# Banks of their own for context blocks and value products, rotations behind the context's product, and a new order of loads in the second layer

## The chip, the cores and the metric

One core of a Trainium2 chip runs the whole program: a model of two layers over 512 latent tokens and 256 context tokens, 1024 channels, batch 1. The metric is the device time of one execution in microseconds (us). The kernel before takes 2702.51 us (median of 3 runs, 2702.22 to 2703.63).

## The reference

All data are float32. The parts that the change touches are the start of each layer and the attention.

```python
for l in range(DEPTH):                                  # DEPTH = 2
    last = l == DEPTH - 1
    sh1, sc1, gt1, sh2, sc2, gt2 = modulation(c, w_mod[l], b_mod[l])
    csh1, csc1, cgt1, csh2, csc2, cgt2 = modulation(c_ctx[None, :], w_mod[l], b_mod[l])
    h_lat = rmsnorm(x, g_norm1[l]) * (1.0 + sc1) + sh1
    h_ctx = rmsnorm(ctx, g_norm1[l]) * (1.0 + csc1) + csh1
    p_lat = h_lat @ w_in[l]
    if last:
        p_ctx_kv = h_ctx @ w_in[l][:, OFF_K:OFF_SC]     # the context's keys and values alone
    else:
        p_ctx = h_ctx @ w_in[l]
        p_ctx_kv = p_ctx[..., OFF_K:OFF_SC]
    k_ctx, v_ctx = keys_values(p_ctx_kv, k_gain[l])     # rmsnorm per head of 128
    q_lat = apply_rope(query_heads(p_lat, q_gain[l]), cos, sin)
    k_lat, v_lat = keys_values(p_lat[..., OFF_K:OFF_SC], k_gain[l])
    k_lat = apply_rope(k_lat, cos, sin)
    attn_lat = latent_attention(q_lat, k_lat, v_lat, k_ctx, v_ctx)
    x_new = x + gt1 * mixer_merge(p_lat, attn_lat, lp)
    h2 = rmsnorm(x_new, g_norm2[l]) * (1.0 + sc2) + sh2
    x_new = x_new + gt2 * squared_relu_mlp(h2, w_mlp_in[l], w_mlp_out[l])
    if not last:
        ...                                             # the same for the context, which reads only itself
    x = x_new
return rmsnorm(x, g_final)
```

There are 8 query heads and 2 key and value heads of 128 channels. The context's keys and queries carry no rotation.

## The kernel before, in words

**Products.** Every float32 operand of a large product is split into a high part (a cast to the matmul's reduced float32) and a low part (the rest), and `mm3` (lines 161 to 165) issues three matmuls for one product: high by high, the two mixed ones, all summed in PSUM. Weights come from HBM in units of 128 x 1024 numbers (512 KB) through four buffers (`wraw`, line 123). ScalarE (ACT) casts a unit (line 134), VectorE (DVE) or GpSimd (POOL) subtracts (line 136); four buffers each for the two parts. `w_qk` (line 475) loads a unit of the first query group's and the keys' columns in two DMAs, `qk_halves` splits it; there are four such units for a layer.

**PSUM.** A `PB` tile is one bank (512 columns, four of them in these stages), a `PA` tile two banks (1024 columns, two of them). In the two stages that matter here TensorE (PE) works with both.

**Other buffers.** SBUF tiles are taken by tag: tag A has 36 buffers, tag X 12 (token rows of 1024 columns, rotary tables, projections, probabilities, each call of `self.X`), tag `gt` (gate rows) 2, tag `gain` 2.

**Who orders.** The program is written as one sequence, partly through generators that are advanced a step at a time between other work (`coming`, `self.lat`, `ctx`, `self.bg`). A planner then sorts each engine's instructions: it simulates the engines, issues what is ready, prefers what is earlier in the program, and allots the tiles' buffers as it goes. `issue_after(x)` ties instructions: they may not be put in their queue before x has been put in its own. On the chip the order of each queue is then fixed. All loads in question stand in SyncE's queue (SP).

**The start of a layer.** Token rows are normalised (`norm_in`, line 1090: ACT sums the squares at 1093, POOL takes the root in `rstd` at 378 and 379, DVE scales at 1095). `modulate` (line 415) transposes the normalised rows on PE (428), and for each block of 128 channels ACT writes the modulated high part (433), ACT or DVE the whole (436 for odd blocks, 438 for even ones), DVE the low part (439). For the two blocks of context tokens a block of channels is 256 columns wide; with `wide` four such blocks share one PA, so two share a bank: one is transposed and read, then the next.

`qk_gemm_all` (line 484) multiplies all four latent blocks with the query and key columns, four banks open at once, and before products it advances `coming`, which is `first_in` in the first layer and `next_in` in the second; these make the modulated rows and the weights just ahead of their use. Then the context's product runs in one PA (lines 582 to 590).

**Rotations.** `rotary_in` (line 454) loads two gains and two copies of the rotary table (512 KB each, tag X). `rotary` (line 468) multiplies the tables by the gains on DVE. `qk_pair` (line 505) sums squares on ACT (512), and on DVE multiplies by the two halves of the table (522) and adds (525); `key` (551) then scales keys on POOL (555), `query` (559) leaves queries unscaled. The latents' two pairs of blocks are rotated ahead of the context's product in the program (lines 579 to 581), the context's pair behind it. `to_heads` (529) transposes the results into heads (534) and splits them.

**Attention.** `v_heads` (line 597) makes the values: three steps, each two products of 256 columns that share a PB bank, each split by ACT and DVE (156, 159). Two of the steps run before the first scores and one more between scores (732, 733, 738). `scores` (628) with part 2 are the context's own queries (first layer only): two products of 256 columns in one PB (651), each read before the next is written.

**Second layer's start.** It overlaps the end of the first layer's MLP. `finish` (1055) normalises each block as its last residual is done; the context's two blocks are the last two. `next_in` (1213) loads the four units of query and key weights, then the rotary tables, splits the weights, multiplies the tables, and modulates latents and context between products.

**Gate rows.** `gate_rows` (364) loads rows that multiply the output of a sub-layer into the residual (`residual`, 1112); the final norm's gain is loaded likewise at 1019. Both are plain loads on SP's queue.

## Time and profile before

| what | value |
|---|---|
| time, median of 3 runs | 2702.51 us (2702.22 to 2703.63) |
| the profiled execution's own time | 2700.5 us |
| its span | 2698.7 us |
| granted TensorE clock, mean over the span | 0.999 |
| PE busy | 2672.6 us |
| PEld busy (weight loads, beside PE) | 2300.5 us |
| DVE busy | 1624.6 us |
| ACT busy | 873.9 us |
| POOL busy | 693.3 us |
| DMA, mean over the span | 112 GB/s |

The profile is of one execution. PE is the engine of the matmuls, PEld its weight loads, DVE the vector engine, ACT the scalar engine, POOL GpSimd, SP the queue that issues most transfers. A line of a view names the line of the source (L163), the operation, and output<-inputs by the names of the tiles, and in brackets how long the engine stood idle ahead of it and what released it.

### The profile page before, as it was taken

How to read it: one execution, taken by the hardware profiler on the slowest of the kernel's cores; microseconds unless marked ns; L12 is line 12 of the kernel's file. 1: busy time of each engine (PE TensorE's matmuls, PEld its weight loads, DVE VectorE, ACT ScalarE, POOL GpSimd, SP SyncE). 2: the span in 40 equal slices, each digit the busy share in tenths (PEclk: the TensorE clock that was granted, in tenths of full speed). 3: DMA queues.
4: the chain of work that ended last, by engine and by line, in shares of the span. 5: the costliest groups of instructions: out<-in, count | busy, mean ns of one | idle time of the engine just before them, and what ended most of it. 6: DMA issues, size and time to landing. Idle time of an engine off the chain costs nothing.

```text
span 2698.7 us, 36188 instructions
## 1 busy us (share of the span) xinstructions
PE 2672.6 (99%) x14571; PEld 2300.5 (85%) x14571; DVE 1624.6 (60%) x2098; ACT 873.9 (32%) x1426; POOL 693.3 (26%) x593
## 2 busy tenths in 40 slices
PE   8999999999999999999999999999999999999998
PEld 5899888888888888888888888998888888888887
DVE  5656837897764335585445356657578645644545
ACT  4556222122212323412121235563223233422223
POOL 1433432243221220201010103335445212111102
PEclk9999999999999999999999999999999999999999
DMA  7211324432275243344334232114333634432332
GB/s 255 64 35 58 98 77 141 133 107 66 82 228 157 63 144 94 97 159 153 110 104 146 79 110 87 55 60 122 120 114 102 181 112 144 132 95 94 110 101 94
DMA packets 341983, 302.50 MB, mean 112 GB/s; under 512 B 10577, under 2 KB 288385, under 8 KB 341817
## 3 DMA queue, kind: packets, MB, share of 16 engines
q1 hardware_dynamic: 340400, 298.81, 35.8%
q8 instruction: 114, 1.87, 0.3%
q10 hardware_dynamic: 1416, 1.39, 0.2%
q14 instruction: 53, 0.43, 0.0%
HBM read 274.96 MB, written 25.20 MB: 111 GB/s over the span
## 4 chain that ended last, share of the span: by engine, by line
PE 96%; DVE 2%; DMA 1%; ACT 1%; issue 0%; POOL 0%; SPq 0%; POOLq 0%; ACTq 0%; DVEq 0%
PE pa L163 21%; PE pa L165 21%; PE pa L164 21%; PE pb L163 9%; PE pb L165 8%; PE pb L164 8%; PE pb L676 2%; PE pb L690 1%; PE pb L693 1%; PE pb L691 1%; DVE tx L522 1%; PE pa L428 0%; DVE wlo L136 0%; PE pb L918 0%; PE pb L784 0%
## 5 line engine op out<-in xcount | busy, mean ns | idle before, releaser
L163 PE MATMUL pa<-ta,whi 128*128 128x512 f32 (+1 forms) x2896 | 1023.9, 354 | 0.0
L164 PE MATMUL pa<-ta,wlo 128*128 128x512 f32 (+1 forms) x2896 | 1020.1, 352 | 0.0
L165 PE MATMUL pa<-ta,whi 128*128 128x512 f32 (+1 forms) x2896 | 1019.6, 352 | 0.0
L134 ACT CAST whi<-wraw 128x1024 fp32r<-128x1024 f32 x360 | 377.8, 1051 | 1036.5 <-PE pa L165 404.3
L163 PEld LDWEIGHTS pa<-ta,whi 128*128 128x128 f32 x2896 | 547.9, 189 | 78.5 <-issue 2.5
L165 PEld LDWEIGHTS pa<-ta,whi 128*128 128x128 f32 x2896 | 547.4, 189 | 75.0 <-DVE ta L439 0.2
L164 PEld LDWEIGHTS pa<-ta,wlo 128*128 128x128 f32 x2896 | 548.0, 189 | 73.4
L163 PE MATMUL pb<-whi,ta 128*128 128x512 f32 (+1 forms) x1200 | 435.2, 363 | 3.5 <-ACT ta L433 1.9
L165 PE MATMUL pb<-wlo,ta 128*128 128x512 f32 (+1 forms) x1200 | 432.5, 361 | 1.5 <-DVE wlo L136 1.5
L164 PE MATMUL pb<-whi,ta 128*128 128x512 f32 (+1 forms) x1200 | 432.9, 361 | 0.0
L760 DVE SCALAR_TENSOR_TENSOR pv<-tx,cols,pv 128x783 f32<-128x783 f32 (+1 forms) x448 | 400.9, 895 | 12.6
L136 DVE TENSOR_TENSOR wlo<-wraw,whi 128x1024 fp32r<-128x1024 f32 x248 | 322.7, 1304 | 89.3 <-ACT whi L134 83.5
L136 POOL TENSOR_TENSOR wlo<-wraw,whi 128x1024 fp32r<-128x1024 f32 x112 | 270.2, 2414 | 360.2 <-ACT whi L134 308.0
L163 PEld LDWEIGHTS pb<-whi,ta 128*128 128x128 f32 x1200 | 226.8, 189 | 41.7 <-ACT ta L433 2.6
L982 POOL TENSOR_TENSOR ta<-ta 128x768 fp32r<-128x768 f32 (+1 forms) x64 | 105.0, 1641 | 600.2 <-DVE ta L981 593.7
L165 PEld LDWEIGHTS pb<-wlo,ta 128*128 128x128 f32 x1200 | 226.7, 189 | 35.2 <-DVE wlo L136 1.7
L164 PEld LDWEIGHTS pb<-whi,ta 128*128 128x128 f32 x1200 | 227.0, 189 | 34.7 <-issue 0.8
L315 DVE SCALAR_TENSOR_TENSOR tx<-wraw,cs,tx 128x1024 f32<-128x1024 f32 x112 | 157.9, 1424 | 49.0 <-DMA wraw<-in_w_mod 44.1
L979 DVE TENSOR_SCALAR ta<-pa 128x512 f32<-128x512 f32 (+1 forms) x63 | 51.8, 822 | 192.5 <-PE pa L165 181.9
L1116 DVE TENSOR_TENSOR ta<-pb,gt 128x512 f32<-128x512 f32 x100 | 68.8, 688 | 160.0 <-PE pb L165 159.9
L803 ACT ACTIVATE ta<-pa 128x768 f32<-128x768 f32 (+1 forms) x52 | 36.6, 705 | 223.8 <-PE pa L165 215.1
L159 POOL TENSOR_TENSOR ta<-tx,ta 128x768 fp32r<-128x768 f32 (+1 forms) x32 | 52.6, 1643 | 156.2 <-ACT ta L156 151.7
(188 smaller groups left out, 2352.0 us busy)
## 6 DMA issues: line engine op xcount, KB each, us to landing
wraw<-in_w_in SPq DMA_DIRECT2D x144, 512.0 KB
wraw<-in_w_mod SPq DMA_DIRECT2D x80, 512.0 KB
wraw<-in_w_mlp_out SPq DMA_DIRECT2D x72, 512.0 KB
wraw<-in_w_mlp_in SPq DMA_DIRECT2D x64, 512.0 KB
wraw<-in_w_o SPq DMA_DIRECT2D x24, 512.0 KB
tx<-spill SPq DMA_DIRECT2D x24, 384.0 KB
ta<-in_w_mod SPq DMA_DIRECT2D x32, 256.0 KB
wraw<-in_w_attn_out SPq DMA_DIRECT2D x16, 512.0 KB
```

What stands on the lines that cost most here:

```text
L134: nc.scalar.copy(hi, raw)
L136: self.last_lo = self.lo_engine.tensor_tensor(lo, raw, hi.bitcast(F32), op=ALU.subtract)
L159: (eng or nc.gpsimd).tensor_tensor(lo, src, hi.bitcast(F32), op=ALU.subtract)
L163: nc.tensor.matmul(ps, ah, bh, start=start, stop=False)
L164: nc.tensor.matmul(ps, al, bh, start=False, stop=False)
L165: self.last_pe = nc.tensor.matmul(ps, ah, bl, start=False, stop=stop)
L315: nc.vector.scalar_tensor_tensor(acc[b], raw, c, acc[b], op0=ALU.mult, op1=ALU.add)
L676: nc.tensor.transpose(pt[:, b * 256 + q * P:b * 256 + (q + 1) * P], probs[n, part][q][:, o], self.ident)
L760: nc.vector.scalar_tensor_tensor((v if t == K_CF - 1 else pv)[:, 0:n], u[:, t:t + n], c["cf"](t, k), (v if t == 1 else pv)[:, 0:n], op0=AL ...
L979: nc.vector.tensor_scalar(out=v[:, 0:n], in0=ps[:, 0:n], scalar1=0.0, scalar2=None, op0=ALU.max)
L982: nc.gpsimd.tensor_tensor(lo[:, 0:n], v[:, 0:n], hi[:, 0:n].bitcast(F32), op=ALU.subtract)
L1116: nc.vector.tensor_tensor(t, ps, gt[:, o], op=ALU.mult)
```

## The change

It has seven parts.

1. `gate_rows` and the load of the final gain are tied behind the last weight load issued so far in the program.
2. `modulate`: for wide blocks of 256 columns, both blocks of a bank are transposed before either is read.
3. `attention`: in the first layer the keys' scaling goes from POOL to ACT; the rotations of both latent pairs (first layer) or of the second pair (second layer) stand behind the context's product; the value weights are asked for ahead of these.
4. `v_heads`: each of the six value products has a PB of its own.
5. `scores`, part 2: both products of a bank are issued before either is read.
6. The third step of the values runs before the first scores in the first layer.
7. `next_in`: gains and rotary tables are loaded first, the eight loads of query and key weights are tied behind the last of the tables, and the tables' multiplication is tied behind the modulation's last subtraction at the fifth block of channels.

```diff
--- before.py
+++ after.py
@@ -123,9 +123,9 @@
         raw = self.W("wraw", N_RAW, shape)
         if isinstance(src, list):
             for k, part in enumerate(src):
-                nc.sync.dma_start(out=raw[:, k].rearrange("p (s c) -> p s c", s=2), in_=part)
+                self.last_load = nc.sync.dma_start(out=raw[:, k].rearrange("p (s c) -> p s c", s=2), in_=part)
         else:
-            nc.sync.dma_start(out=raw, in_=src)
+            self.last_load = nc.sync.dma_start(out=raw, in_=src)
         return raw
 
     def halves(self, raw, shape):
@@ -366,7 +366,8 @@
         got = []
         for b in range(nb):
             t = self.small.tile([P, D], F32, name="gt", tag="gt", bufs=2)
-            self.nc.sync.dma_start(out=t, in_=self.gates[l, r][b:b + 1, :].broadcast_to([P, D]))
+            with self.tc.issue_after(self.last_load.ins):
+                self.nc.sync.dma_start(out=t, in_=self.gates[l, r][b:b + 1, :].broadcast_to([P, D]))
             got.append(t)
         return got
 
@@ -420,12 +421,17 @@
             if wide and not pre and j % (1024 // n) == 0:
                 pa = self.PA()
             at = j % (1024 // n) * n
+            bank = 512 // n if wide else 1
             if pre:
                 ps = pre.pop(0)
             else:
+
                 ps = pa[:, at:at + n] if wide else self.PB()
-                for q, xn in enumerate(xns):
-                    nc.tensor.transpose(ps[:, q * P:(q + 1) * P], xn[:, j * P:(j + 1) * P], self.ident)
+                to = pa[:, at:] if wide else ps
+                for u in range(bank if j % bank == 0 else 0):
+                    for q, xn in enumerate(xns):
+                        nc.tensor.transpose(to[:, u * n + q * P:u * n + (q + 1) * P],
+                                            xn[:, (j + u) * P:(j + u + 1) * P], self.ident)
             a = self.scale[l][:, which, b, j:j + 1]
             s0 = 0 if which == 0 else 24
             sh = self.mc[l][:, b, s0 + j:s0 + j + 1]
@@ -461,7 +467,7 @@
             gains.append(g)
         for g in gains:
             rope = self.X(D)
-            nc.sync.dma_start(out=rope, in_=i["rope"])
+            self.last_rope = nc.sync.dma_start(out=rope, in_=i["rope"])
             ropes.append(rope)
         self.tables = gains, ropes
 
@@ -552,8 +558,12 @@
             t, ss = self.qk_pair(t, p, gains[0], ropes[0])
             r = self.rstd(ss[:, 0:4], 4, 1.0 / P, EPS)
             for q in range(4):
-                nc.gpsimd.tensor_scalar(out=t[:, q * P:(q + 1) * P], in0=t[:, q * P:(q + 1) * P],
-                                        scalar1=r[:, q:q + 1], scalar2=1.0, op0=ALU.mult, op1=ALU.mult)
+                o = slice(q * P, (q + 1) * P)
+                if l == 0:
+                    nc.scalar.activation(t[:, o], t[:, o], AF.Copy, scale=r[:, q:q + 1])
+                else:
+                    nc.gpsimd.tensor_scalar(out=t[:, o], in0=t[:, o], scalar1=r[:, q:q + 1], scalar2=1.0,
+                                            op0=ALU.mult, op1=ALU.mult)
             heads.append((t, p, kt))
 
         def query(g, t, p, apart=False):
@@ -576,7 +586,9 @@
         kt = self.new_pairs(2)
         new_queries(0)
         gains, ropes = self.tables
-        for p, (tk, tq) in enumerate(pairs):
+        pairs = list(enumerate(pairs))
+        late = pairs[0 if l == 0 else 1:]
+        for p, (tk, tq) in pairs[:len(pairs) - len(late)]:
             key(tk, p)
             query(0, tq, p)
         pa = self.PA()
@@ -588,22 +600,23 @@
                 c = slice((NB_L + b) * P, (NB_L + b + 1) * P)
                 self.mm3(ps[b][:, o], hs[k][0][:, c], hs[k][1][:, c], ws[k][0][:, o], ws[k][1][:, o],
                          k == 0, k == KT - 1)
-        tk, tq = self.qk_out(ps, full)
-        key(tk, 2)
-        if full:
-            query(0, tq, 2)
+        late.append((2, self.qk_out(ps, full)))
+        w_v = self.w_rows(w, 0, OFF_V, 256)
+        for p, (tk, tq) in late:
+            key(tk, p)
+            if tq is not None:
+                query(0, tq, p)
         vt = self.new_pairs(2)
 
         def v_heads():
-            ws = self.w_rows(w, 0, OFF_V, 256)
+            ws = w_v
             for p in range(3):
-                ps = self.PB()
                 for b in range(2):
-                    blk = 2 * p + b
-                    self.gemm_tm(ps[:, b * 256:(b + 1) * 256], ws, hs, blk)
+                    blk, ps = 2 * p + b, self.PB()
+                    self.gemm_tm(ps[:, 0:256], ws, hs, blk)
                     hi, lo = vt[blk // 3]
                     o = slice((blk % 3) * 256, (blk % 3 + 1) * 256)
-                    self.split(ps[:, b * 256:(b + 1) * 256], hi[:, o], lo[:, o], eng=nc.vector)
+                    self.split(ps[:, 0:256], hi[:, o], lo[:, o], eng=nc.vector)
                 yield True
 
         spill = [self.spill([P, T]) for _ in range(8)]
@@ -648,7 +661,9 @@
                     p = self.A() if part else self.X(T)
                 else:
                     sv = s[:, q * TC:(q + 1) * TC]
-                    self.mm3(sv, qh[:, o], ql[:, o], kh[:, TL:T], kl[:, TL:T], True, True)
+                    for u in range(2 if q == 0 else 0):
+                        c = slice((blk + u) * P, (blk + u + 1) * P)
+                        self.mm3(s[:, u * TC:(u + 1) * TC], qh[:, c], ql[:, c], kh[:, TL:T], kl[:, TL:T], True, True)
                     p = self.X(TC)
                 a = 4 * q
                 nc.vector.tensor_reduce(out=m[:, a:a + 1], in_=sv, axis=AX.X, op=ALU.max)
@@ -729,8 +744,8 @@
 
         items = 2 * len(parts)
         vg = v_heads()
-        next(vg)
-        next(vg)
+        for _ in range(3 if l == 0 else 2):
+            next(vg)
         with self.tc.issue_after(self.last_pe.ins):
             later(0)
         for _ in range(LEAD):
@@ -1017,7 +1032,8 @@
             self.bg.append(nxt)
         else:
             gf = self.small.tile([P, D], F32, name="gt", tag="gt", bufs=2)
-            nc.sync.dma_start(out=gf, in_=i["g_final"][None, :].broadcast_to([P, D]))
+            with self.tc.issue_after(self.last_load.ins):
+                nc.sync.dma_start(out=gf, in_=i["g_final"][None, :].broadcast_to([P, D]))
             self.g_final = gf
             self.ys = {}
         self.lo_engine = nc.vector
@@ -1213,15 +1229,18 @@
     def next_in(self, ws):
 
         l = DEPTH - 1
-        raws = [self.w_qk(self.i["w_in"][l], u) for u in range(KT // 2)]
         self.rotary_in(l)
+        with self.tc.issue_after(self.last_rope.ins):
+            raws = [self.w_qk(self.i["w_in"][l], u) for u in range(KT // 2)]
         for raw in raws:
             ws += self.qk_halves(raw)
-        self.rotary()
         ctx = self.ctx_in(l)
         for k in range(KT):
             for _ in range(4 if k == 0 else 1):
                 next(self.lat, None)
+            if k == CTX_FROM:
+                with self.tc.issue_after(self.last_dve.ins):
+                    self.rotary()
             for _ in range(CTX_STEP if k >= CTX_FROM else 0):
                 next(ctx, None)
             yield True
```

## Rows read from the trace of the kernel before

**Rows 1.** The page, busy time of each engine: us (share of the span), instructions

```profile
PE 2672.6 (99%) x14571; PEld 2300.5 (85%) x14571; DVE 1624.6 (60%) x2098; ACT 873.9 (32%) x1426; POOL 693.3 (26%) x593
```

**Rows 2.** Windows: us, then PE, PEld, DVE, ACT, POOL busy, PEclk, DMA, GB/s

```profile
57.00:260.00 203.00, 197.51 (x1486) 185.46 (x1485) 133.78 (x296) 125.06 (x348) 80.79 (x97) 1.00 0.16 48
1600.00:1800.00 200.00, 195.08 (x1371) 178.87 (x1370) 138.46 (x255) 120.01 (x286) 67.77 (x76) 1.00 0.24 74
```

**Rows 3.** Timeline of PE, first layer: start, us, engine, line, tiles, count [idle before]

```profile
64.39 0.44 PE L428 MATMUL pa<-ident,tx 128*128 128x128 f32 x2 [0.88 <-ACT ta L436]
...
65.32 0.39 PE L163 MATMUL pb<-whi,ta 128*128 128x256 f32 x1 [0.50 <-ACT whi L134]
...
69.62 0.44 PE L428 MATMUL pa<-ident,tx 128*128 128x128 f32 x2 [0.80 <-DVE ta L438]
...
70.56 0.50 PE L164 MATMUL pa<-whi,ta 128*128 128x512 f32 x1 [0.49 <-DVE ta L439]
...
85.81 0.39 PE L163 MATMUL pb<-whi,ta 128*128 128x256 f32 x1 [0.92 <-DVE ta L159]
```

**Rows 4.** Timeline of PE at the second layer's start

```profile
1623.64 0.40 PE L163 MATMUL pb<-whi,ta 128*128 128x512 f32 x1
1623.88 0.39 PE L164 MATMUL pb<-whi,ta 128*128 128x512 f32 x1
...
1637.89 0.44 PE L428 MATMUL pa<-ident,tx 128*128 128x128 f32 x2 [0.99 <-DVE ta L438]
...
1659.62 0.38 PE L165 MATMUL pb<-wlo,ta 128*128 128x256 f32 x1 [1.45 <-DVE wlo L136]
```

**Rows 5.** Timeline of PE, first layer: transposes of heads, and a context score

```profile
88.80 1.91 PE L534 MATMUL pb<-ident,tx 128*128 128x128 f32 x16
...
252.59 0.39 PE L163 MATMUL pb<-ta 128*128 128x256 f32 x1
```

**Rows 6.** Timeline of SP's queue (SPq)

```profile
1058.06 1.10 SPq L952 DMA_DIRECT2D tx<-in_ctx  x2
...
1607.56 7.69 SPq L126 DMA_DIRECT2D wraw<-in_w_in  x8
...
1624.17 1.29 SPq L369 DMA_DIRECT2D gt<-spill  x1
...
1628.23 0.98 SPq L464 DMA_DIRECT2D tx<-in_rope  x2
```

**Rows 7.** Timeline of DVE

```profile
1060.16 0.75 DVE L961 TENSOR_SCALAR tx<-tx,st 128x1024 f32<-128x1024 f32 x1 [1.79 <-POOL st L397]
...
1629.06 0.75 DVE L1095 TENSOR_SCALAR tx<-tx,st 128x1024 f32<-128x1024 f32 x1 [0.72 <-POOL st L379]
...
1634.91 2.46 DVE L472 TENSOR_TENSOR tx<-tx,gain 128x1024 f32<-128x1024 f32 x2 [4.51 <-DMA tx<-in_rope]
```

**Rows 8.** Timeline of ACT at the second layer's start

```profile
1621.15 2.94 ACT L134 CAST whi<-wraw 128x1024 fp32r<-128x1024 f32 x3
...
1625.97 1.03 ACT L1093 ACTIVATE pa<-tx 128x1024 f32<-128x1024 f32 x1 [1.21 <-DVE tx L1117]
```

**Rows 9.** Windows, columns as in group 2

```profile
22.00:30.00 8.00, 4.96 (x17) 3.42 (x16) 5.25 (x12) 3.68 (x5) 0.00 (x0) 0.79 1.10 350
73.00:89.00 16.00, 15.08 (x112) 14.25 (x111) 7.58 (x12) 7.13 (x26) 13.01 (x21) 1.00 0.45 135
1623.00:1637.00 14.00, 13.90 (x64) 10.96 (x63) 8.76 (x11) 4.93 (x8) 1.73 (x2) 1.00 0.78 261
```

**Rows 10.** Groups by shape, 57 to 90 us: count | busy us, mean ns | idle before

```profile
L522 DVE TENSOR_TENSOR tx<-tx 128x512 f32<-128x512 f32 x8 | 5.3, 681 | 0.0
...
L136 DVE TENSOR_TENSOR wlo<-wraw,whi 128x1024 fp32r<-128x1024 f32 x4 | 4.9, 1221 | 2.0 <-ACT whi L134 2.0
...
L433 ACT ACTIVATE ta<-pa,mc,scale 128x256 fp32r<-128x256 f32 x6 | 3.4, 565 | 2.5 <-PE pa L428 2.5
L436 ACT ACTIVATE ta<-pa,mc,scale 128x256 f32<-128x256 f32 x3 | 1.7, 557 | 0.0
```

## The prediction

> **What bounds the kernel now.** I read the page first: TensorE is busy 2672.6 of 2698.7 us [rows 1], so any gain has to come out of the 26 us in which it stands, or out of stalls too short to show as idle. Next, the sums by stage: in 57 to 260 us (first layer's start and attention) PE misses 203.00 - 197.51 = 5.5 us, in 1600 to 1800 (second layer's start) 4.9 us [rows 2]. The rest lies in stages where the change adds or removes no wait of note, the kernel's two ends above all. Then PE's own timeline in the two stages names each gap and who ended it [rows 3, 4]; last, the queues of SP, DVE and ACT at the second layer's start, because the change rearranges loads there [rows 6 to 8], with two sums by window [rows 9] and groups by shape [rows 10] for durations. A bracketed idle understates a stall: a 128x512 product lasts 0.40 us in a row but starts 0.23 to 0.24 before the next (1623.64, 1623.88) [rows 4], so I add 0.2 us to each.
>
> **Context blocks in one bank, first layer.** Four waits lie in the context's product: 0.88 and 0.80 us before transposes (until ACT and DVE have read the other half of the bank), 0.50 before the first value product (the cast of its weights), 0.49 before a product (DVE's low part, queued behind rotations) [rows 3]. The change writes both halves before either is read, asks for the value weights earlier, and puts the rotations behind the product. All four answers are direct: 2.67 + 4 x 0.2 = **3.4 us** go. Bounds 0 (other work of DVE takes the place) and 3.4; I take 3.4, since each wait is undone by its own edit.
>
> **Value products in banks of their own.** 0.92 + 0.2 = **1.1 us** go in the first layer (the second half waited for the split of the first) [rows 3]; in the second layer no such idle shows, 0 to 0.2.
>
> **Scores of the context, first layer.** One half's first product waits until the other half of its bank is read. The row at 252.59 is such a one; it shows no idle, so by the margin above at most 0.2 us is lost [rows 5]. Eight heads: 0 to 1.6 us; most show less than this one, so I take **0.4**.
>
> **Rotations moved, keys on ACT, third value product moved.** No operation is added. The rotations of four latent tiles are 8 multiplications of 0.681 us and four additions of the same shape: 8.2 us of DVE [rows 10] that would now run beside the value products. In 73 to 89 us DVE is busy 7.58 of 16 [rows 9]: 7.58 + 8.2 = 15.8, a tight cover, but some of the rotations still fit into DVE's gaps before. If the cover fails, the transposes of the heads come late: 0 to 2 us. Scaling the first layer's keys goes from POOL, busy 13.01 of these 16 us, to ACT, busy 7.13 [rows 9]; nobody on PE waits for either now, so 0. The third value product leaves the score stage some 5.8 us of PE work (48 products of 256 columns, half of 0.23 to 0.24 apart) poorer; the next query's products are the cover, price if they aren't enough 0 to 1.5 us. I take 0 for the three and keep 0 to +3.5.
>
> **Second layer's waits.** The transpose at 1637.89 waited 0.99 us for DVE, which had just been held by the two gain multiplications of the rotary table (2.46 us, begun only when the table landed, 4.51 us idle before) [rows 4, 7]. These move behind the modulation: 1.2 us. The low part of the value weights (1.45 us, 1659.62) stood behind the second pair's rotations; the pair moves behind the product: 1.65. Together **2.9 us** go (bounds 0 and 2.9: each wait can be replaced by a smaller one).
>
> **Gate rows behind the last weight load.** The planner issues loads as early as a buffer allows: a gate row of the second layer, needed only behind its mixers, took 1.29 us of SP's queue at 1624.17 [rows 6]. Moved, these come some tens of us before their use; PE waits for no weight load in these stages, and the first residual of a stage follows four weight units later. Cost 0; if the cover is gone, one row's landing, some 3 to 6 us (two 512 KB tables took 6.7 us from issue at 1628.23 to use at 1634.91 [rows 6, 7]).
>
> **Rotary table ahead of the query and key weights, second layer.** This is the part that decides. Now the eight weight loads go out from 1607.56, are through on SP at 1615.3, and the table goes out only at 1628.23 [rows 6], though it depends on nothing computed. So what it waited for was a buffer. It lives in tag X (12 buffers), and at 1610 no more than eight X tiles are in use (two residual streams, six normalised copies), so the buffers were not full. The same shows in the first layer: the two context rows, inputs too, were issued only at 1058.06, in between the normalised copies of the latents, one of which follows at 1060.16 [rows 6, 7], though four of 12 were free. I read from this that buffers of a tag are given in program order: the table cannot be placed before the last normalised copy (context block 1, the L1095 at 1629.06) has its buffer. With the change the weight loads are tied behind the table. On the chip SP may run ahead of that plan, but ACT's and DVE's written order may not: the casts of these weights, which stand at 1621.15 and before today, ahead of the last sum of squares at 1625.97 [rows 8], come behind it, and behind what else the planner finds ready while it waits for the loads: the context's modulation.
>
> Price: today the product starts at 1623.64 without a break [rows 4]. The last normalised copy ends at 1629.06 + 0.75 = 1629.8; without the weight subtraction between its steps (1.22 [rows 10]) and with POOL's steps less disturbed I put it at 1627.9. Then 0.4 for the first transposes; the context's modulation on ACT is 8 x 0.565 + 4 x 0.557 = 6.7 us [rows 10], of which I set three quarters, 5.0, before the first cast; a cast of 1.0 (2.94 for three [rows 8]) and a subtraction of 1.2. That is 1635.5; two products (0.45) run before the subtraction. So PE loses 1635.5 - 0.45 - 1623.64 = 11.4 us, less the 16 context transposes that fall into it anyway (0.11 each, as 16 transposes in 1.91 us with the last one's tail [rows 5]: 1.75): **9.7 us**. Bounds: below, a cast right behind the sum of squares (about 1626.1 + 1.0 + 1.2 - 0.45 - 1623.64 = 4.2 us; 0 if my reading of the buffers is wrong). Above, loads that really leave only at 1627.9: 6.7 for the table, 2.0 for 512 KB of weights at the 261 GB/s of that stretch [rows 9], cast and subtraction: 1638.8 - 0.45 - 1623.64 - 1.75 = 13.0 us.
>
> The clock: in 22 to 30 us PE was busy 4.96 of 8 us, with gaps of some us, and its granted clock was 0.79 of full on average: at the lower of its two levels (1.2 against 2.4 GHz) for (1 - 0.79) x 2 x 8 = 3.4 us [rows 9]; products in that time take double, 1.7 us lost. The gap forecast here is longer than those, so I add **1.7 us** (0 to 3.4). The Trainium skill, "TensorE: Matmul & The Clock Gate", section "What's actually happening", has it that the throttled clock is the default and activity releases it; the trace agrees (those 3.4 us). By that rule the term stays, without it the sum would be 1.7 us less.
>
> **Sum.** -3.4 - 1.1 - 0.4 - 2.9 + 9.7 + 1.7 = +3.6 us on the profiled execution (2700.5 us, 1.8 of them outside the span): 2704.1. The median shown, 2702.51, is 2.0 above that execution, so the prediction is **2706.1 us** as a median: no change, or just slower. About 0.2%, 5.4 us, is what a measurement here can tell from no change.
>
> **Rivals.** (a) *The table doesn't hold the weights up*: the planner finds it a buffer early, the product starts as now. For it: SP's queue runs ahead of any plan, X buffers are free. Against: the table's place in the queue at 1628.23. Then -7.8: 2694.7 us, faster. (b) *The loads really leave late and the moved rotations too*: the upper bounds, 13.0 + 1.7 for the weights and up to 2 for heads that come late in the first layer: -7.8 + 16.7 = +8.9, 2711.4 us, slower. It decides from the point where the table's buffer is one that a late reader still holds (the residual stream that L1095 reads at 1629.06), so that SP itself waits. For it: nothing tells which buffer is taken; against: buffers long free exist. (c) *The gains don't come*: waits only change place, gains of 3 instead of 7.8, and casts right behind the sum of squares: +4.2 - 3 = +1.2, 2703.7, inside my forecast's own range.
>
> **How the numbers follow.** My forecast (with c) 0.61: from -7.8 + 4.2 = 2698.9 to 2711; rival (a) 0.17; rival (b) 0.22. Faster than 2697.1: nearly all of (a) and little else, 0.17. Slower than 2707.9: (b), and a quarter of my own case, 0.36. Within: 0.47. The range reaches to both rivals: 2694.5 to 2712.
>
> **What would show it.** In the trace after: a gap of PE at the second layer's start (1615 to 1640 us), ended by a cast or subtraction of query and key weights, with the clock lower behind it; the table's loads ahead of the eight weight loads on SP. No idle before context transposes or between the value products in the first layer. If PE runs through the second layer's start without a gap, (a) holds and my reading of the buffers was wrong. If waits of 0.5 us and more show at the heads' transposes near 90 us, the moved rotations were not covered.

## The result: slower by 0.54%, and the profile after

The changed kernel takes 2718.72 us (median of 6 runs, 2712.49 to 2721.16), the kernel before 2702.67 in the same comparison: a ratio of 1.0054, interval 1.0044 to 1.0064. I had forecast 2706.1 in a range of 2694.5 to 2712.0: the sign of my sum was right, the size far off. The profiled execution (2721.16 us, span 2719.1, clock 0.994) is the slowest of the six. Its busy times, which answer to [rows 1]:

```profile
PE 2680.6 (99%) x14571; PEld 2308.2 (85%) x14571; DVE 1626.2 (60%) x2098; ACT 876.7 (32%) x1438; POOL 677.7 (25%) x581
```

The work is the same, but for 12 scalings that went from POOL to ACT (581 and 1438 instructions); PE is busy 8.0 us longer with the same 14571 instructions. Where the time went is read by comparing when PE starts the same instruction in the two traces:

| the same instruction of PE | before | after | shift | this stage |
|---|---|---|---|---|
| transpose of the column table, L244 | 56.94 | 57.92 | +1.0 | +1.0 |
| the context's last high product of 512 columns | 76.25 | 73.74 | -2.5 | -3.5 |
| the ninth latent score of 512 columns | 135.25 | 140.85 | +5.6 | +8.1 |
| a product of the convolution stage | 509.75 | 518.02 | +8.3 | +2.7 |
| column sums of a modulation, L327 | 575.17 | 587.18 | +12.0 | +3.7 |
| a product of the first layer's MLP | 1565.24 | 1577.21 | +12.0 | 0.0 |
| the second layer's last latent score | 1793.09 | 1813.73 | +20.6 | +8.6 |
| end of the span | 2698.7 | 2719.1 | +20.4 | -0.2 |

Windows of the kernel after (us, then PE, PEld, DVE, ACT, POOL busy, PEclk, DMA share, GB/s); the first three together answer to the first of [rows 2], the last to its second:

```profile
57.00:84.00 27.00, 27.00 (x167) 23.88 (x166) 20.05 (x35) 17.98 (x57) 4.12 (x6) 1.00 0.27 79
84.00:130.00 46.00, 40.17 (x273) 37.17 (x272) 28.00 (x63) 26.03 (x86) 14.42 (x19) 0.89 0.09 25
130.00:268.00 138.00, 135.82 (x1052) 128.13 (x1051) 86.11 (x201) 85.02 (x220) 48.77 (x62) 1.00 0.14 47
1600.00:1820.00 220.00, 208.96 (x1418) 190.79 (x1417) 142.63 (x261) 122.58 (x290) 67.67 (x80) 0.98 0.22 68
```

PE runs through the context's product without a gap, as forecast; then, in 84 to 130 us, it stands for 5.8 of 46 us, and its clock is 0.89. The stalls there and at 568 us, from PE's timeline, beside which the waits of [rows 3] are gone:

```profile
90.73 1.03 PE L540 MATMUL pb<-ident,tx 128*128 128x128 f32 x8
92.03 0.66 PE L540 MATMUL pb<-ident,tx 128*128 128x128 f32 x4 [0.26 <-DVE ta L159]
94.90 1.12 PE L540 MATMUL pb<-ident,tx 128*128 128x128 f32 x4 [2.21 <-DVE ta L159]
...
110.28 0.66 PE L540 MATMUL pb<-ident,tx 128*128 128x128 f32 x4 [1.93 <-DVE tx L531]
...
568.71 0.75 PE L163 MATMUL pa<-ta,whi 128*128 128x512 f32 x1 [1.90 <-DVE tx L813]
```

L540 are the transposes of the heads: they wait for DVE's split of the heads ahead (L159), the last ones for the rotation of the next queries (L531). DVE's timeline shows what stood in front of those splits:

```profile
92.15 2.36 DVE L136 TENSOR_TENSOR wlo<-wraw,whi 128x1024 fp32r<-128x1024 f32 x2 [0.18 <-ACT whi L134]
94.43 2.94 DVE L159 TENSOR_TENSOR ta<-pb,ta 128x256 fp32r<-128x256 f32 x8
```

Those are the low parts of the third query group's weights, which before stood at 106.49 and 110.35, behind the splits. At the second layer's start SP, ACT and PE answer to [rows 6], [rows 8] and [rows 4]:

```profile
1611.93 1.19 SPq L470 DMA_DIRECT2D tx<-in_rope  x2
1619.53 7.69 SPq L126 DMA_DIRECT2D wraw<-in_w_in  x8
```

```profile
1636.19 1.03 ACT L1109 ACTIVATE pa<-tx 128x1024 f32<-128x1024 f32 x1 [0.30 <-DVE tx L1133]
...
1644.72 0.56 ACT L442 ACTIVATE ta<-pa,mc,scale 128x256 f32<-128x256 f32 x1
1645.17 1.04 ACT L134 CAST whi<-wraw 128x1024 fp32r<-128x1024 f32 x1
```

```profile
1636.87 0.85 PE L433 MATMUL pa<-ident,tx 128*128 128x128 f32 x5 [1.79 <-DVE ta L444]
1639.09 0.98 PE L433 MATMUL pa<-ident,tx 128*128 128x128 f32 x7 [1.37 <-DVE tx L1111]
1641.92 1.12 PE L433 MATMUL pa<-ident,tx 128*128 128x128 f32 x4 [1.85 <-ACT ta L442]
1646.26 0.79 PE L163 MATMUL pb<-whi,ta 128*128 128x512 f32 x1 [3.22 <-ACT whi L134]
```

The loads left early and were through on SP at 1627.2; their casts stand in ACT's queue behind the last sum of squares and part of the context's modulation, and PE's first product waits for the first cast. Last, the clock (windows of the kernel after, columns as above):

```profile
90.00:100.00 10.00, 7.53 (x40) 6.31 (x39) 7.61 (x16) 6.99 (x22) 1.70 (x2) 0.72 0.37 108
110.00:115.00 5.00, 4.72 (x24) 4.51 (x25) 3.15 (x9) 2.43 (x5) 1.81 (x2) 0.66 0.02 5
568.00:573.00 5.00, 4.29 (x12) 3.41 (x13) 4.87 (x6) 2.63 (x4) 2.36 (x1) 0.66 0.23 60
1635.00:1647.00 12.00, 3.77 (x19) 2.66 (x19) 9.69 (x16) 8.41 (x15) 0.74 (x2) 0.73 0.00 1
1647.00:1660.00 13.00, 13.00 (x51) 10.56 (x50) 4.78 (x6) 3.36 (x5) 0.00 (x0) 0.85 0.52 161
```

(1 - clock) x length is the full-speed time missing: 2.8 + 1.7 + 1.7 + 3.2 + 2.0 = 11.4 us, part of it while PE stood anyway. Before, both windows of the first layer were all at 1.00 (windows of the kernel before):

```profile
57.00:84.00 27.00, 24.33 (x141) 20.33 (x140) 22.43 (x38) 18.10 (x69) 20.94 (x19) 1.00 0.27 80
84.00:130.00 46.00, 43.33 (x338) 41.18 (x337) 27.61 (x62) 25.23 (x68) 12.33 (x19) 1.00 0.09 25
```

### The profile page after: what moved, and what is told of

Read it like the earlier page. It is cut to its first block, busy times and chain, and to the rows that moved or that the text cites. A ratio compares the mean times of both kernels' runs of the same rounds, so it can differ in the third digit from the quotient of the medians.

```text
span 2719.1 us, 36170 instructions
## 1 busy us (share of the span) xinstructions
PE 2680.6 (99%) x14571; PEld 2308.2 (85%) x14571; DVE 1626.2 (60%) x2098; ACT 876.7 (32%) x1438; POOL 677.7 (25%) x581
## 4 chain that ended last, share of the span: by engine, by line
PE 87%; DVE 2%; ACT 1%; issue 0%; POOL 0%; POOLq 0%; ACTq 0%; DVEq 0%
PE pa L163 20%; PE pa L164 20%; PE pa L165 20%; PE pb L163 8%; PE pb L164 8%; PE pb L165 8%; PE pb L691 1%; DVE tx L315 1%; DVE pv L775 1%; PE pb L705 1%; PE pb L708 1%; PE pb L706 0%; PE pa L433 0%; PE pb L933 0%; PE pb L799 0%
## 5 line engine op out<-in xcount | busy, mean ns | idle before, releaser
L159 POOL TENSOR_TENSOR ta<-tx,ta 128x768 fp32r<-128x768 f32 (+1 forms) x32 | 52.5, 1641 | 156.4 <-ACT ta L156 152.0
```

Of the source, the lines that this page charges most:

```text
L159: (eng or nc.gpsimd).tensor_tensor(lo, src, hi.bitcast(F32), op=ALU.subtract)
```

## The experiments

Every run is compared with the kernel before, whose median lay between 2702.45 and 2702.78 us. "84 to 130 us loses" in the expectations is the sum over PE's products of start to next start, less their spacing in an unbroken row (0.227 us at 512 columns, 0.120 at 256, 0.109 for a transpose): 3.9 us before, 11.8 after. The table gives this sum for each run's profiled execution, and for 57 to 84 us (the context's product) beside it.

| run | median us | ratio (interval) | 57 to 84 us loses | 84 to 130 us loses |
|---|---|---|---|---|
| kernel before | 2702.67 | 1 | 4.1 | 3.9 |
| changed kernel | 2718.72 | 1.0054 (1.0044 to 1.0064) | 0.5 | 11.8 |
| e1: weights loaded first again | 2708.16 | 1.0020 (1.0011 to 1.0029) | 0.5 | 10.9 |
| e6: tables placed early | 2708.22 | 1.0019 (1.0010 to 1.0028) | 0.5 | 10.9 |
| e2: third value step between scores | 2716.71 | 1.0050 (1.0038 to 1.0063) | 0.4 | 10.7 |
| e5: before + three bank edits | 2707.32 | 1.0017 (1.0008 to 1.0026) | 6.9 | 3.1 |
| f1: before + context blocks by two | 2705.81 | 1.0012 (1.0002 to 1.0021) | 6.7 | 3.9 |
| f2: before + value banks | 2700.46 | 0.9992 (0.9983 to 1.0002) | 3.6 | 2.7 |
| f3: before + paired scores | 2707.31 | 1.0015 (1.0006 to 1.0024) | 4.1 | 4.2 |
| f4: e6 + rotations first | 2711.48 | 1.0031 (1.0019 to 1.0044) | 6.3 | 6.5 |
| g3: f4 + third value step between scores | 2705.26 | 1.0009 (1.0000 to 1.0018) | 6.5 | 3.9 |
| g2: e6 + third group's low parts on POOL | 2704.83 | 1.0009 (1.0000 to 1.0018) | 0.5 | 8.3 |
| f5: e6 + keys on POOL | 2705.39 | 1.0009 (1.0000 to 1.0018) | 0.5 | 10.3 |
| h1: late rotations, costly parts out | 2702.60 | 1.0001 (0.9992 to 1.0010) | 0.5 | 10.2 |
| h2: h1 + values first, low parts on POOL | 2699.07 | 0.9985 (0.9976 to 0.9995) | 0.5 | 6.8 |
| g1: value banks + second layer's parts | 2698.82 | 0.9986 (0.9977 to 0.9994) | 3.6 | 2.7 |

Two runs whose intervals overlap are not told apart by time alone; for e2 against the changed kernel, f4, g2 and f5 against e6, h1 against g1 and h2 against h1 they overlap, and the traces have to carry the reading. Parts 1 (gate rows) and 3's early value weights were not run alone; where the gate rows are used, the table of stages shifts by 0.0 and -0.2 us.

**e1 and e6, the second layer's loads.** Two ways out of the gap, the changed order undone (e1) or kept with the tables asked for earlier (e6):

```diff
-        self.rotary_in(l)
-        with self.tc.issue_after(self.last_rope.ins):
-            raws = [self.w_qk(self.i["w_in"][l], u) for u in range(KT // 2)]
+        raws = [self.w_qk(self.i["w_in"][l], u) for u in range(KT // 2)]
+        self.rotary_in(l)
```

> The changed kernel, but at the second layer's start the query and key weights are loaded ahead of the rotary tables again, as before; all else as changed. Theory A (the casts of these weights stand in ACT's queue behind the context's modulation, because the tables that the loads are tied to get a buffer only after the last normalised copy): the gap that ends with the cast at 1646.26 us goes, and the 7.0 us that 1625 to 1700 us lost against before turn into some 3 gained: 2718.7 - 10 = 2709 us (2707 to 2712). Rival B (the second layer loses by the later multiplication of the tables and the later rotations, which stay here): 2716 to 2719 us, and gaps of 1 us and more stay between the transposes of the context.

```diff
@@ next_in
-        self.rotary_in(l)
@@ finish, where h == int(b < NB_L)
+            if b == 0:
+                self.rotary_in(l + 1)
             self.norm_in(b, x, self.X(), self.PA())
```

> The changed kernel, but the rotary tables of the second layer are asked for in the program when the first latent block of the first layer is finished, ahead of the later normalised copies; the weight loads stay tied behind the tables. Theory A (the tables got their buffer late because buffers of a tag are given in program order): the planner places tables and weights early, casts run ahead of the last sum of squares again, and the gap before the second layer's first product goes: 2709 us (2706 to 2712). Rival B (the tie itself holds the weights up, whenever the tables get their buffer): 2717 to 2720 us.

Both give back 10.5 us, theory A's number. In e1 one wait of 2.10 us stays before transposes of the context (1650.74). In e6 the casts stand on both sides of a sum of squares again (ACT), and no idle of PE shows in 1600 to 1660 us:

```profile
1628.48 1.03 ACT L1111 ACTIVATE pa<-tx 128x1024 f32<-128x1024 f32 x1 [0.29 <-DVE tx L1135]
...
1629.54 1.03 ACT L134 CAST whi<-wraw 128x1024 fp32r<-128x1024 f32 x1
1631.81 2.94 ACT L134 CAST whi<-wraw 128x1024 fp32r<-128x1024 f32 x3
1636.64 1.03 ACT L1111 ACTIVATE pa<-tx 128x1024 f32<-128x1024 f32 x1 [1.20 <-DVE tx L1135]
```

The tie to the tables is still there; only the place where the program asks for the tables has changed, and their loads now leave at 1489.00 and 1491.91. That this place decides is so shown, and the rival of the tie falls. Whether it decides by the order in which buffers are given, or because the planner prefers what is earlier in the program, no run tells apart.

**e2, the third value step** (`for _ in range(2)` in place of 3 in the first layer).

> The changed kernel, but the third step of the values runs between scores again, as before, in the first layer too. Theory A (this step is what costs the first layer: without it between scores nothing covers the split of the heads and the next queries' rotation, and the query weights' subtraction gets ahead of the heads' splits on DVE): the waits of 2.2 us at 94.90 and 1.9 us at 110.28 and the low clock behind both go, some 9 us: 2709.5 us (2707 to 2713). Rival B (the rotations behind the context's product make the heads late, whatever the values do): the wait at the heads' transposes stays, 2716 us or more.

Theory A failed: 2 us, inside the intervals, and the time is in rival B's band. The two waits went, and two others came: 1.31 us for a split, then 3.79 for the first score, as the heads are not ready. So the values' place was not the cause by itself.

**e5, f1, f2, f3, the bank edits** added to the kernel before, together and one by one (their diffs are parts 2, 4 and 5 of the change).

> The kernel before with the three bank edits alone: both context blocks of a bank transposed before either is read, a bank for each value product, both context scores of a bank issued before either is read. The prediction's terms for these are 0.88 + 0.80 + 0.92 us and three margins of 0.2, and 0.4 for the scores, 3.6 us in all: 2699.1 us (2698 to 2700.5). Rival: the waits only change place (DVE is the engine that ends them in either order): 2702.2 to 2703 us.

> The kernel before with one edit: both context blocks of a bank are transposed before either is read. Theory A (the waits only change place here: with the rotations between them, ACT and DVE reach the second block of a bank no earlier, and the four transposes at once then wait for the slower reader): the first layer's stretch of the context's product (57 to 84 us) loses some 2 to 3 us more than before, the second layer's start loses 1 to 2 less: 2703 to 2705 us. Rival B (the prediction's term: 0.88 + 0.80 us and two margins of 0.2): 2700.4 us.

> The kernel before with one edit: a bank for each value product. Theory A (a value step takes two of four banks, and the transposes and scores beside it in the first and second layer wait longer for a free one): 1 to 2 us are lost at 1700 to 1800 us, 0.9 us gained between the value products of the first layer: 2703 to 2704.5 us. Rival B (the prediction's term, 0.92 + 0.2 us gained): 2701.4 us. Rival C (this edit, by its banks, makes the waits that come back every second head from 170 us on): 2705 to 2707 us.

> The kernel before with one edit: both products of a context score bank are issued before either is read. Theory A (the second product moves ahead of the projection of the next queries, and what waits for these probabilities, the transposes and value products, loses that cover): waits of 0.8 and 0.4 us come back at every second head from 170 us on, some 3 us in 130 to 330 us: 2705 to 2706.5 us. Rival B (the prediction's term, 0.4 gained): 2702.1 us.

Together they cost 4.9 us where the terms for these edits had 3.6 gained; 2707.3 is above the rival's band too. The value banks gain 2.2, with an interval that just reaches no change; of the three theories rival B (1.1 gained) is the nearest. Context blocks by two cost 3.2 with the rotations in place, of which the trace has 2.6 in 57 to 84 us, as theory A has it; PE and ACT of f1:

```profile
68.56 0.66 PE L431 MATMUL pa<-ident,tx 128*128 128x128 f32 x4 [2.73 <-ACT ta L440]
```

```profile
67.22 0.29 ACT L516 ACTIVATE tx<-tx 128x128 f32<-128x128 f32 x1
67.42 0.19 ACT L516 ACTIVATION_READ_ACCUMULATOR tx<-tx 128x1 f32 x1
67.51 0.54 ACT L437 ACTIVATE ta<-pa,mc,scale 128x256 fp32r<-128x256 f32 x1
67.96 0.55 ACT L440 ACTIVATE ta<-pa,mc,scale 128x256 f32<-128x256 f32 x1
```

Between 62.83 and 67.51 ACT does nothing but the rotations' sums of squares and one cast, and the second block's modulation stands behind them: the bank had been waiting for ACT's queue, not for a turn. Paired scores cost 4.7 us by the medians. The trace has 3.0 of it where they act: 130 to 510 us loses 6.0 us in every kernel with paired scores and 3.0 in every one without. Beside that f3 loses 1.9 us more in 510 to 600 us, where no such scores run. The second product now runs ahead of the next queries' projection, and the transposes and value products that need the probabilities lose that cover. The two waits come back once, 46.8 us later (213.39 and 215.03):

```profile
166.56 0.36 PE L692 MATMUL pb<-tx,ta 128*128 128x256 f32 x1 [0.64 <-DVE st L660]
...
168.20 0.63 PE L534 MATMUL pb<-ident,tx 128*128 128x128 f32 x4 [0.26 <-DVE tx L159]
```

**f4, g3, g2, f5: the first layer's start, one part at a time, on e6.**

```diff
-        late = pairs[0 if l == 0 else 1:]
+        late = pairs[2 if l == 0 else 1:]
```

> The changed kernel with its tables placed early (as in the run whose time was 2708.2 us), and with the first layer's rotations of latents ahead of the context's product again. Theory A (rotations behind the product make the heads late, wherever the values run): the 11 us that 84 to 130 us loses fall to 4 to 5, the context's product loses 6 to 7 us instead of 0.5: 2707 to 2709 us in all, so that the order of the rotations only moves the loss. Rival B (the heads are late because nothing is left to cover their split, with the third value step gone): 84 to 130 us still loses 9 to 11 us, 2712 us or more.

With the rotations first the loss of 84 to 130 us fell to 6.5, between the two theories, and the context's product lost 6.3, as theory A has it; the median is above its band, the profiled execution (2707.21, the fastest of its six) in it. The wait for the next queries' rotation (1.93 us at 111.92) stayed.

g3 adds `for _ in range(2)` to f4:

> The changed kernel with its tables placed early, with the first layer's rotations ahead of the context's product (so far 2711.5 us), and with the third value step between scores again. Theory A (once the heads are early, the value products between scores cover the split of the heads and the next queries' rotation, as in the kernel before): the waits of 1.3 us at the heads' transposes and 1.9 us at the next queries' heads go, 84 to 130 us loses 3 to 4 us instead of 6.5: 2708 us (2707 to 2710). Rival B: the values' place is worth 2 us or less, as it was with the rotations late: 2709.5 to 2711.5 us.

It gave 6.2 us by the medians, more than either theory. The traces show about half of it: 84 to 130 us loses 2.7 us less, and the two profiled executions (2707.21 and 2703.92) are 3.3 us apart. The wait for the queries' rotation is gone; this window of g3 answers to the one of 0.89 above.

```profile
84.00:130.00 46.00, 43.40 (x339) 41.21 (x339) 28.87 (x66) 27.87 (x87) 14.15 (x17) 1.00 0.14 41
```

g2 takes the two subtractions off DVE:

```diff
+            lo, self.lo_engine = self.lo_engine, nc.gpsimd if l == 0 and g == 2 else self.lo_engine
             ws = self.w_rows(w, 0, g * 256, 256)
+            self.lo_engine = lo
```

> The changed kernel with its tables placed early (2708.2 us), and with the low part of the third query group's weights made on POOL, which is idle for 11.75 us there, instead of DVE. Theory A (these two subtractions, 2.36 us at 92.15, stand ahead of the heads' splits and cause the wait of 2.2 us at 94.90 and the low clock behind it): 84 to 130 us loses some 4 to 5 us less: 2704 us (2702.5 to 2705.5). Rival B (the heads come late for the rotations alone, and another wait takes the place): 2707 us or more.

The time is in theory A's band, but 84 to 130 us loses only 2.6 us less, not 4 to 5. The wait of 2.21 us fell to 1.16, at the place that theory A named, and the queries' wait is unchanged; PE of g2:

```profile
93.65 0.66 PE L540 MATMUL pb<-ident,tx 128*128 128x128 f32 x4 [1.16 <-DVE ta L159]
94.66 0.51 PE L163 MATMUL pa<-ta 128*128 128x512 f32 x1 [0.35 <-ACT ta L156]
106.64 1.06 PE L540 MATMUL pb<-ident,tx 128*128 128x128 f32 x4 [1.93 <-DVE tx L531]
```

What is left of the first wait hangs on ACT: the casts of the same two weight units stand ahead of the heads' casts (L156), for which DVE's splits wait. In the changed kernel they stand there too (91.07), before the change behind the heads (105.41 and 106.62). ACT of g2:

```profile
90.89 1.99 ACT L134 CAST whi<-wraw 128x1024 fp32r<-128x1024 f32 x2
92.78 0.90 ACT L156 CAST ta<-pb 128x256 fp32r<-128x256 f32 x3
```

f5 scales the keys on POOL as before:

> The changed kernel with its tables placed early (2708.2 us), and with the first layer's keys scaled on POOL again. Theory A (the prediction: nobody on PE waits for this scaling on either engine): 2708.2 us within 1. Rival B (ACT's queue stands 0.8 and 1.0 us for POOL's roots ahead of the scaling, and the sums of squares and casts behind it come later): 2705.5 to 2707 us with the keys on POOL. Rival C (POOL's scaling makes the heads still later): 2709.5 us or more.

Nearly rival B's number, 2.8 us gained, but the cause is not shown. Its profiled execution was the slowest of its ten (2708.94) and shows 10.3 us lost in 84 to 130 us instead of e6's 10.9, so the trace doesn't show where the rest of the 2.8 came from.

**h1 and h2, are late rotations a loss of their own?** h1 is e6 with single scores, keys on POOL and the third value step between scores; h2 is h1 with that step ahead again and g2's edit.

> The changed kernel without the parts that the runs showed to cost: tables placed early, context scores one by one, keys on POOL, third value step between scores. Beside the version of 2698.8 us it differs in the first layer alone: context blocks two by two, the latents' rotations behind the context's product, value weights asked for early. Theory A (with the rotations late the heads come late, and what 57 to 84 us gains, 3.1 us, 84 to 130 us loses twice over): 2701.5 us (2700 to 2704). Rival B (the losses of the first layer came from the other parts, and late rotations are a gain of their own): 2694 to 2697 us.

> The same, but with the third value step ahead of the first scores, as changed, and the low part of the third query group's weights on POOL (2.36 us less on DVE among the heads' splits). Theory A (the third value step covers the late heads, but then the next queries' rotation is uncovered, 2 us and the clock behind it): 2700.5 us (2699 to 2703). Rival B (the value step ahead of the scores pays once DVE is relieved): 2695 to 2698 us.

h1 is 3.8 us slower than g1. They differ in the first layer's late rotations, paired context blocks and early value weights, and, which the expectation leaves out, in the ties of the gate rows and of the second layer's weights; these do not show there (PE is busy 217.20 us of 1600 to 1820 in h1 and 217.21 in g1). By the traces h1 gains 3.1 us against g1 in 57 to 84 us and loses 7.5 in 84 to 130 us. The rotations make the heads late, here by way of POOL, whose first four scalings take 4.04 us; e2, with the keys on ACT, lost as much at the same place:

```profile
81.85 4.04 POOL L565 TENSOR_SCALAR tx<-tx,st 128x128 f32<-128x128 f32 x4
```

```profile
89.61 0.48 PE L540 MATMUL pb<-ident,tx 128*128 128x128 f32 x1 [2.90 <-POOL tx L565]
```

h2 is as fast as g1, with 6.8 us lost in 84 to 130 us instead of h1's 10.2. It has two edits more than h1, so how much is the value step's and how much that of the relieved DVE is not shown. What is left is mostly the queries' wait and the clock behind it:

```profile
105.33 0.66 PE L540 MATMUL pb<-ident,tx 128*128 128x128 f32 x4 [1.93 <-DVE tx L531]
```

**g1, put together from these:** value banks; and in the second layer alone blocks by two (`if wide and l > 0`), late rotation of the second pair, late tables, early value weights, and e6's early place of the tables.

> A version put together from what the runs showed: the kernel before, with a bank for each value product, and in the second layer alone the context's blocks transposed two at a time, the second pair's rotation and the tables' multiplication late, the value weights asked for early, and the rotary tables asked for when the first latent block is finished. Theory A (the two gains add: 2.2 us of the value banks, and 1.2 to 2.9 us of waits in the second layer): 2698.5 us (2697 to 2700). Rival B (the second layer's waits only move to the first scores): 2700.5 us, as with the value banks alone.

It is 0.14% faster than the kernel before, as theory A has it; from f2 alone the time does not tell it apart. Its window, and that of the kernel before, against 208.96 us of PE in the kernel after:

```profile
1600.00:1820.00 220.00, 217.21 (x1499) 199.50 (x1498) 146.87 (x265) 129.70 (x300) 74.75 (x87) 1.00 0.24 73
1600.00:1820.00 220.00, 215.08 (x1487) 196.59 (x1486) 143.35 (x262) 129.65 (x300) 74.05 (x86) 1.00 0.24 74
```

## Why the prediction was wrong, step by step

- **Rotary table ahead of the weights: right.** Forecast 9.7 + 1.7 for the clock, less 2.9 of gains: 8.5. The stage lost 8.6, and e1 and e6, which take the gap away, gave 10.5. The mechanism was the one told: loads early on SP, casts late on ACT, and all of it from the place where the program asks for the tables; that buffers are the reason stays an inference. Rival (a) falls by the gap, rival (b) by the loads: they left at 1619.53, which is the 1607.56 of before and the 12.0 us that the kernel was behind. The lower bound's 1626.1 is in no row (the sum of squares of [rows 8] ends at 1627.0), but nothing hung on it.
- **Second layer's waits: right in size.** 2.9 forecast; in g1, without the gap, 1600 to 1820 us loses 6.0 us instead of 8.9. Some 0.8 of these 2.9 come with the value banks (f2).
- **Context blocks in one bank: right size for the whole, wrong reason.** The stage gained 3.5 for a forecast of 3.4, but not since "each wait is undone by its own edit": f1 shows a loss of 3.2 with the banks alone. It was the move of the rotations out of ACT's and DVE's queues that freed the stage: with them first again it loses 6.3 instead of 0.5 (f4 against e6).
- **Rotations moved, keys on ACT, third value product moved: the step that failed.** I took 0 (to +3.5) where the stage, for which I had 1.1 of gain, lost 8.1. My cover counted DVE's busy share (7.58 + 8.2 of 16 us) and was true in sum: the rotations did fit in (DVE is busy 11.43 us of 73 to 89 us after the change). What was late is the chain behind them (rotation, root, scaling, transpose, split), with 2.36 us of weights sorted in among the splits and 1.99 us of their casts ahead of them (g2). And the third value step, which I had hidden behind "the next query's products", was itself what covered the next queries' rotation (g3 against f4: 2.7 us of the window). With early heads the step is needed between the scores. With late heads its place alone decides little: 10.7 us lost between the scores (e2), 11.8 ahead of them. The scaling of keys on ACT may have cost something too: 2.8 by f5's median, of which the trace shows 0.7. The sign that the prediction names for an uncovered move came: a wait of 2.21 us at the heads' transposes (94.90).
- **Scores of the context: wrong sign.** 0.4 gained in the forecast; alone they lost 4.7 by the medians (f3), 3.0 of it in the trace where they act (2.7 in the table of stages). I looked at the wait for the bank, and not at what PE's queue runs in that time: the projection that it now runs later.
- **Value products: right.** 1.1 forecast; in f2's trace 84 to 130 us loses 2.7 us instead of 3.9, and the 2.2 of the medians is not told apart from that. For the second layer I had 0 to 0.2; 1600 to 1820 us loses 0.8 less in the same trace.
- **The clock** was in my sum for the second layer alone. In the first it came with three waits of some 2 us: 2.8 + 1.7 + 1.7 us in the three windows.
- **Open:** the wait for L813 near 568 us (1.90 us and the clock behind it, 3.7 in the table). By the same sum 510 to 600 us loses 1.8 to 3.8 us more than in the kernel before in all eight kernels whose latent rotations are late and in e5, f1 and f3, and nothing more in f2, f4, g3 and g1: late rotations go with it each time, but no single edit explains it. The 1.0 us ahead of 57 us, where transposes at 51.48 wait for a copy, also differs among runs whose edits lie elsewhere. No run was made for either.

## What to carry to other kernels

A wait for a bank ends when the reader's queue comes to it: before giving it another bank, read what stands ahead of the reader. Where order is sorted by a planner, an instruction moved away from a place also takes its cover from there; look for who ran beside it, and count the chain behind a moved step, not the engine's free share. Tying loads to another load ties the work behind them to the place where the program asks for that one.

## What the runs showed of the hardware that was not expected

Short waits can cost nearly as much again by the clock. After PE stood 2.21 us (94.90), 1.93 (110.28) and 1.90 (568.71), products of 256 columns start 0.21 us apart instead of 0.12, or ones of 512 columns 0.43 instead of 0.23, until 3.5 to 6.3 us after the wait; in windows around them the granted clock is 0.72, 0.66 and 0.66, so in part at the lower of its two levels. It does not follow each time: the clock stays at 1.00 behind a wait of 2.11 us at 51.48 in the same trace, and behind f4's of 1.93 us at 111.92. The spread of the changed kernel's runs goes with the same thing: 2712.49 us at a mean clock of 0.997, 2721.16 at 0.994, and 0.003 x 2719 = 8.2 of these 8.7 us; with clocks known to three decimals it may be 5.4 to 10.9, and part of that time PE stood anyway.
